# Other instruction durations in the planner that orders a hybrid SSD and attention layer on one core

## The chip, the core and the metric

The kernel runs on one core of one Trainium2 chip. A core has TensorE (matrix products, transposes as products with an identity, weight loads), VectorE (DVE in the rows), ScalarE (ACT), GpSimd (POOL) and SyncE (SP), which here issues all DMAs. The metric is device microseconds of one execution, as the median of several runs. Before the change it is 1239.81 us over 3 runs (1235.19, 1240.91 and 1239.81).

## The reference

For x of 1024 tokens times 1024 channels in float32:

```python
h = layer_norm(x, ln_emb_g, ln_emb_b)
proj = einsum("bsd,de->bse", h, w_in)                # 6688 columns
z, xbc, dt_f, dt_b, q, k, v, g = split(proj)
xbc = silu(centred_dwconv(xbc, conv_w, conv_b))      # 5 taps
y = ssd(forward) + ssd(backward) + D * xs            # 16 heads, 2 groups, 8 chunks of 128 tokens
y_ssm = rms_norm(y * silu(z))                        # per group
w = softmax(s1 - m_h|t-s|) - lam * softmax(s2 - m_h|t-s|)   # 8 heads, two maps each
y_attn = rms_norm(w @ v) * 0.8 * silu(g)
mix = concat([y_ssm, y_attn]) @ w_out
out = layer_norm(ALPHA * h + mix, ln_g, ln_b)
```

## The kernel before

**Products.** Large products are made in float32r, with both operands split into a rounded high part and the remainder: three matmuls of 128x128 by 128x512 stand for one full product (high by high, high by low, low by high). The input projection is 52 blocks of 128 columns; a block is 2 halves of the sequence times 8 slices of 128 channels times 3 matmuls, 48 in all. Transposes, the SSD products and the chunk states are plain float32.

**Lanes.** The work is written as generators, called lanes. `fill` makes the projection blocks one after the other, `weights` loads and splits their weights. In the SSD part `conv`, `states` (the recurrence over chunks, with its state tile H), `maps`, `diag` (products of the within-chunk maps, tile t) and `gate` run for group 0 and then for group 1. In the attention part `scores` makes 128 queries of one head at a time (8 matmuls into the tile sc, for two maps), `combine` subtracts the normalised maps, `values` transposes and splits the result (wh, wl) and multiplies it by the values. `finish` normalises a head. At the end `rows_out`, `y_out`, `residuals` and `project_out` make the output projection: 16 units of 48 matmuls, the first 8 (part 0) on the SSD half, the last 8 (part 1) on the attention half. Part 0 of token blocks 6 and 7 waits for the last head's scores, and part 1 for the last head to be finished.

**The planner.** `Loom.run` decides, while the program is being built, in which order the lanes' instructions are emitted. Every call through an `Engine` wrapper is priced by a cost function (`_pe_cost`, `_dve_cost`, `_act_cost`, `_pool_cost`, `_dma_cost`, in us) and entered by `Loom.note` in a table of when each tile is written. TensorE's clock of the planner is the sum of the prices of what has been emitted on it. On the other engines `Loom.slot` puts an instruction into the first gap that takes it. A lane that yields a tile goes on when the planner's TensorE clock has reached the time the tile is ready plus the lane's margin, from the table LANES (0.2 to 3 us). Among lanes that are ready, the lowest rank goes first:

```python
k = (max(ln[0], now), ln[1], ln[2])          # ready time or now, rank, age
...
ln[0] = ln[5] + max(self.ready.get(t, 0.0) for t in _tiles(...))   # ln[5] is the margin
```

`fill` and the lanes of the output projection have rank 9, the highest number, so they are what TensorE gets while the others wait. All TensorE instructions, and the DVE and ACT ones issued through `VO` and `AO`, keep the order in which they were emitted; other instructions of DVE, ACT and POOL are placed by the framework. The planner never sees the chip: when a price is too low, an instruction of TensorE is emitted whose operand is not there yet on the chip, and TensorE, which works in order, waits.

**What feeds what.** The scores of a head need its q and k blocks. The q and k blocks of head h wait for the scores of head h-2 (`free_since`), its v block for that head's sums, its gate block for its end. At most two sets of maps are between `scores` and the transposes of `values`.

Of the kernel before, what the change touches and what calls it, by code (L numbers as in the profile page):

```python
# [14 lines left out]
ALU = mybir.AluOpType  # L15
PSUM = bass.MemoryType.PSUM
DRAM = bass.MemoryType.DRAM

S = 1024
# [7 lines left out]
ALPHA = 2.0 ** 0.25  # L27
# rank of each lane, and how much later than estimated it takes its inputs to be ready
LANES = dict(weights=(0, 0.8), channels=(1, 1.2), steps=(2, 1.6), z_tail=(2, 0.8), conv=(3, 1), v_tail=(3, 0.4), states=(4.4, 0.8), diag=(4.125, 0.6), maps=(4.4, 0.6), gate=(4.375, 0.2), finish=(4.2, 2), scores=(4, 0.8), combine=(4.125, 0.6), values=(4.25, 0.4), fill=(9, 0.8), rows_out=(9, 0.2), y_out=(9, 3), residuals=(9, 2), project_out=(9, 2))
# [10 lines left out]
def _width(ap):  # L40
    n = 1
    for s in ap.shape[1:]:
        n *= s
    return n


class Loom:
    """Weaves lanes of work into one instruction order.

    A lane is a generator that emits instructions and yields in between: nothing (it can go on),  # L50
    a tile (it can go on once the tile's last write is done), a function (once it holds) or a
    time (it lets other lanes go first for so long).
    When each tile is ready is estimated from the instructions emitted so far; the lane that
    goes on is the first one, by rank, that would not make TensorE wait."""

# [29 lines left out]
    def slot(self, key, start, cost):  # L85
        """The first gap of an engine that takes an instruction ready at start."""
        busy = self.busy.setdefault(key, [])
        i = len(busy)
        while i and busy[i - 1][1] > start:
            i -= 1  # L90
        while i < len(busy) and busy[i][0] - start < cost:
            start = max(start, busy[i][1])
            i += 1
        busy.insert(i, (start, start + cost))
        del busy[:-300]
        return start
# [33 lines left out]
class Engine:  # L130
    """An engine whose instructions are noted in the loom."""

# [20 lines left out]
class Pool:  # L153
    """A tile pool whose slots' reuse is noted in the loom; under are the pools whose place it takes."""

# [19 lines left out]
def _pe_cost(op, out, ins, func=None):  # L175
    n = _width(out)
    if op == "transpose":
        return 0.107
    if ins[0].dtype == F32R:
        return max(0.107, n * 0.000417 + 0.003)  # L180
    return max(0.214, n * 0.00167)


def _dve_cost(op, out, ins, func=None):
    n = _width(out)
    if op == "reciprocal":
        return 0.06 + n * 0.0083
    if op in ("bn_stats", "tensor_reduce"):
        return 0.06 + _width(ins[0]) * 0.00105
    fast = op in ("tensor_scalar", "tensor_copy") and ins[0].space != PSUM  # L190
    return 0.07 + n * (0.00055 if fast else 0.00105)

# [4 lines left out]
def _act_cost(op, out, ins, func=None, state=[None]):  # L197
    cost = 0.12 + _width(out) * 0.00083
    table = _table.get(func, state[0])
    if table != state[0]:  # L200
        state[0] = table
        cost += 1.3
    return cost


def _pool_cost(op, out, ins, func=None):
    if op == "tensor_scalar":
        return 0.07 + _width(out) * 0.001
    return 0.07 + _width(out) * (0.00225 if func is not ALU.pow else 0.4)

# [6 lines left out]
def hybrid_layer_kernel(  # L217
# [8 lines left out]
    loom = Loom(tc)  # L226
    T = Engine(loom, nc.tensor, "PE", _pe_cost, pinned=True)
    V = Engine(loom, nc.vector, "DVE", _dve_cost)
    A = Engine(loom, nc.scalar, "ACT", _act_cost)
# [25 lines left out]

# [1 line left out]
    ident = const.tile([128, 128], F32, name="ident")  # L257
# [7 lines left out]

    # -|query - key| for every offset of a block of 128 queries
    dist = const.tile([128, 1920], F16, name="dist")

# [1 line left out]
    cols = const.tile([128, 104], F32, name="cols")  # L270
# [6 lines left out]

# [1 line left out]
    h_hi = [[hp.tile([128, 512], F32R, name=f"hh{h}_{k}") for k in range(KB)] for h in range(2)]  # L279
# [16 lines left out]
    class Block:  # L296
        """128 projected channels; evac(half, psum) takes each half of the sequence."""

# [7 lines left out]
    def weights():  # L306
        """Loads and splits the weights of a block while the one before it is computed."""
        for n in range(NB):
            yield lambda: len(queue) > n
            b = queue[n]  # L310
            if b.w:
                continue
            before = queue[n - 1]
            yield lambda: before.begun > 0
            sts = []
            for i in range(2):
                st, src = stage_w(b.col, i, wp, 2)
                yield st
                dma(st, src)
                sts.append(st)  # L320
            if not before.pair:
                yield lambda: before.begun > 1
            for st in sts:
                hi, lo = places_w()
                yield (st, hi)
                b.w.append(split_w(st, hi, lo))
# [40 lines left out]

    # ================= embedding LayerNorm and bidirectional SSD =================
    g0x = px.enter_context(ExitStack())
# [29 lines left out]
    def conv_block(b, when, dst_of, after):  # L399
        """Block b of x/B/C: raw projection, then convolution and SiLU into dst_of()."""  # L400
        hold = {}
# [30 lines left out]
    def to_tokens(src, put):  # L432
        """Transposes src [128 ch, S]; put(half, psum [128 tokens, 4, 128])."""
        for half in range(2):
            pt = bank((128, 4, 128))
            yield (src, pt)
            for j in range(4):
                c = 4 * half + j
                transpose(pt[:, j, :], src[:, 128 * c:128 * c + 128])
            put(half, pt)  # L440
# [41 lines left out]
    with tc.tile_pool(name="dp", bufs=1) as dp_, tc.tile_pool(name="p0", bufs=1) as p0_:  # L482
# [93 lines left out]
        def steps_lane():  # L576
            """Step sizes, decays and their sums within chunks."""
            for half in range(2):
# [80 lines left out]
        first = []  # L659
# [35 lines left out]
    def ssd(g):  # L695
# [72 lines left out]
        def maps():  # L768
            """Within-chunk maps of one head, four chunks at a time."""
            loaded = []  # L770
# [94 lines left out]

    # ================= differential attention =================
    ex = px.enter_context(ExitStack())
# [15 lines left out]
    def free_since(h, what, n):  # L883
        """The tiles that head h overwrites are read no more."""
        if h == 0 and what != "done":
            return None
        if h < 2:
            return lambda: state["open"]
        return lambda: getattr(heads_[h - 2], what) == n
# [87 lines left out]
    def scores():  # L977
        """Unnormalised maps of 128 queries at a time."""
        for h, H in enumerate(heads_):
# [32 lines left out]
    def combine():  # L1012
        """Difference of the two normalised maps, left in the first."""
        for _ in range(64):
# [14 lines left out]
    def values():  # L1029
        """Maps transposed and split; weighted sums of the values, 256 queries at a time."""  # L1030
        for _ in range(64):
# [34 lines left out]
    def finish(H, o, half):  # L1066
        """RMS norm over the head's 128 channels, gate, store."""
        h = heads_.index(H)
# [33 lines left out]

    # ================= output projection and LayerNorm =================
    NE = 5
    last = heads_[7]

    def late_rows():
        """Places for the rows of the attention half: tiles of the last head, as they fall free."""
        for tag, shape, bufs, when in (
# [14 lines left out]
    def early_rows():  # L1124
        """The rows for the SSD half take the place of the normalised input."""
        for i in range(16):
            half, j = i // 8, i % 8
            yield lambda: h_used[half] > j
            yield tuple(hp.tile([128, 512], F32R, name=f"o{c}{i}", tag=f"h{c}{half}_{j}") for c in "hl")
# [3 lines left out]
    def rows_out():  # L1133
        """Splits the rows of the output projection, half a row at a time."""
        yield lambda: h_used[0] > 0
# [27 lines left out]
    def y_out():  # L1163
        """Splits the gated outputs of one unit, two units ahead of the products."""
        for tb, part in units:
# [19 lines left out]
    def residuals():  # L1185
        """ALPHA times the normalised input, token blocks in the order of their use."""
        yield lambda: "pool" in res
# [53 lines left out]
    def project_out():  # L1241
        """One unit is 128 tokens times half of the rows; the first NE blocks leave PSUM in between."""
        acc = {}
# [70 lines left out]
```

## Time and profile before

| | |
|---|---|
| median of 3 runs | 1239.81 us (1235.19 to 1240.91) |
| span of the profiled execution | 1236.1 us; the profile has no other time for it |
| instructions | 16398 |
| PE busy | 1176.0 us, 95% |
| PEld busy | 922.4 us, 75% |
| DVE busy | 933.8 us, 76% |
| ACT busy | 677.8 us, 55% |
| POOL busy | 479.9 us, 39% |
| mean granted TensorE clock | 0.990 |

PE is the matmul side of TensorE, PEld its weight loads, which overlap the matmuls. A matmul's length in the trace is its latency; how far apart matmuls follow one another is read from their start times. The granted clock is a share of full speed, averaged over a stretch. All instructions recorded by the wrappers carry one line, 140, so groups are told apart by their tiles. "bk" and "sb" are banks of PSUM.

### The profile page before, as it was taken

What the parts mean: (1) busy time and instruction counts of PE and PEld (TensorE: products, weight loads), DVE (VectorE), ACT (ScalarE), POOL (GpSimd) and SP (SyncE); (2) the same over time, 40 slices, a digit from 0 to 9 for tenths busy, and PEclk for the clock granted to TensorE, in tenths of its full rate; (3) what the DMA queues carried; (4) which work ended last, traced back from release to release, by engine and by line L of the source; (5) the groups of instructions that cost most, each with busy time, mean ns of one, the idle gap of its engine ahead of it and who ended that gap; (6) DMA issues with size and microseconds to landing.
All of it is one profiled execution on the core that took longest, in us unless ns stands there. A gap on an engine that the chain in (4) does not pass through costs nothing. (4 is left out here: it accounts for less than half of the span.)

```text
span 1236.1 us, 16398 instructions
## 1 busy us (share of the span) xinstructions
PE 1176.0 (95%) x5881; PEld 922.4 (75%) x5881; DVE 933.8 (76%) x1334; ACT 677.8 (55%) x1181; POOL 479.9 (39%) x404
## 2 busy tenths in 40 slices
PE   5998999899899999999999999999999998999997
PEld 3787666788567777777787777877777776778885
DVE  6687888867988568788788787887878889962334
ACT  4556356734457456665755656556656687641221
POOL 7422664323654323223332333233332429541354
PEclk9999999999899999999999999999999998999999
DMA  6113335522245421012112111121111263233221
GB/s 198 32 33 112 89 112 167 178 69 65 89 118 151 132 72 49 26 44 51 26 35 52 43 44 35 34 52 35 43 28 47 81 209 107 55 123 112 78 85 60
DMA packets 107591, 98.03 MB, mean 79 GB/s; under 512 B 9364, under 2 KB 79349, under 8 KB 107509
## 3 DMA queue, kind: packets, MB, share of 16 engines
q1 hardware_dynamic: 107509, 96.98, 27.2%
q8 instruction: 46, 0.75, 0.2%
q14 instruction: 36, 0.29, 0.1%
HBM read 75.85 MB, written 16.91 MB: 75 GB/s over the span
## 5 line engine op out<-in xcount | busy, mean ns | idle before, releaser
L140 PE MATMUL bk<-hh,whi 128*128 128x512 f32 x832 | 353.2, 425 | 0.6
L140 PE MATMUL bk<-hl,whi 128*128 128x512 f32 x832 | 327.0, 393 | 3.2 <-POOL hl L140 2.8
L140 PE MATMUL bk<-hh,wlo 128*128 128x512 f32 x832 | 328.0, 394 | 0.0
L140 ACT ACTIVATE p<-p,nm 128x1024 f32<-128x1024 f32 x128 | 146.8, 1148 | 121.7 <-DVE nm L140 121.0
L140 POOL TENSOR_TENSOR wlo<-wst,whi 128x512 fp32r<-128x512 f32 x104 | 161.5, 1557 | 126.9 <-ACT whi L140 109.2
L140 POOL TENSOR_SCALAR p<-p,rs 128x1024 f32<-128x1024 f32 x56 | 64.5, 1152 | 350.4 <-DVE rs L140 287.5
L140 PEld LDWEIGHTS bk<-hh,wlo 128*128 128x128 f32 x832 | 156.6, 188 | 34.9
L140 PEld LDWEIGHTS bk<-hl,whi 128*128 128x128 f32 x832 | 157.7, 190 | 32.9 <-POOL hl L140 5.4
L140 PEld LDWEIGHTS bk<-hh,whi 128*128 128x128 f32 x832 | 157.7, 190 | 32.7 <-issue 5.8
L140 DVE CUSTOM_DVE_ANT_0 p<-sc,dist 128x1024 f32<-128x1024 f32 x128 | 151.3, 1218 | 11.6 <-PE sc L140 10.9
L140 DVE SCALAR_TENSOR_TENSOR p<-p,rs,p 128x1024 f32<-128x1024 f32 x64 | 128.4, 2007 | 22.1 <-POOL p L140 18.0
L140 DVE TENSOR_TENSOR wl<-bk,wh 128x512 fp32r<-128x512 f32 x128 | 87.0, 684 | 15.6 <-ACT wh L140 13.7
L140 ACT CAST wh<-bk 128x512 fp32r<-128x512 f32 x128 | 74.1, 580 | 43.2 <-PE bk L140 42.7
L140 ACT CAST whi<-wst 128x512 fp32r<-128x512 f32 x104 | 64.2, 620 | 46.9 <-PE bk L140 38.1
L140 PE MATMUL bk<-ident,p 128*128 128x128 f32 x512 | 79.4, 278 | 4.7 <-DVE wl L140 2.7
L140 PEld LDWEIGHTS bk<-ident,p 128*128 128x128 f32 x512 | 61.6, 142 | 29.5 <-DVE wl L140 6.2
L140 PE MATMUL bk<-wh,vh 128*128 128x256 f32 x256 | 74.6, 291 | 0.0
L140 PE MATMUL bk<-wl,vh 128*128 128x256 f32 x256 | 72.2, 282 | 0.7 <-DVE wl L140 0.7
L140 PE MATMUL sc<-kk,q 128*128 128x512 f32 x256 | 72.3, 393 | 0.0
L140 PE MATMUL bk<-wh,vl 128*128 128x256 f32 x256 | 72.0, 281 | 0.0
L140 ACT ACT_TABLE_LOAD x42 | 53.9, 1283 | 25.5 <-DVE t L140 15.7
L140 PEld LDWEIGHTS bk<-xt,t 128*128 128x128 f32 x256 | 45.8, 192 | 26.5 <-issue 15.0
(217 smaller groups left out, 2188.1 us busy)
## 6 DMA issues: line engine op xcount, KB each, us to landing
wst<-in_w_in_dram SPq DMA_DIRECT2D x104, 256.0 KB, 3.0
t<-acs_d SPq DMA_DIRECT2D x64, 256.0 KB, 3.5
ws<-in_w_out_dram SPq DMA_DIRECT2D x32, 256.0 KB, 3.1
ys<-yd SPq DMA_DIRECT2D x32, 256.0 KB, 3.0
xb<-in_x_dram SPq DMA_DIRECT2D x8, 512.0 KB, 6.2
zd<-zs SPq DMA_DIRECT2D x16, 256.0 KB, 2.5
gz<-zd SPq DMA_DIRECT2D x16, 256.0 KB, 3.3
yd<-ys SPq DMA_DIRECT2D x16, 256.0 KB, 2.8
```

Source lines behind the costliest of these rows:

```text
L140: r = f(*args, **kw)
```

## The change

The four cost functions for TensorE, DVE, ACT and POOL get other numbers. The comments and docstrings are taken out as well (as empty lines, so that line numbers stay). LANES, the lanes themselves, `_dma_cost` and everything that is computed stay as they are; only the order in which the planner emits instructions can differ.

```diff
 def _pe_cost(op, out, ins, func=None):
     n = _width(out)
     if op == "transpose":
-        return 0.107
+        return 0.11
     if ins[0].dtype == F32R:
-        return max(0.107, n * 0.000417 + 0.003)
-    return max(0.214, n * 0.00167)
+        if ins[0].shape[0] == 64:
+            return 0.14
+        return max(0.107, n * 0.00043 + 0.009)
+    return max(0.166, n * 0.00168)
...
     if op == "reciprocal":
-        return 0.06 + n * 0.0083
+        return 0.06 + n * 0.0068
     if op in ("bn_stats", "tensor_reduce"):
-        return 0.06 + _width(ins[0]) * 0.00105
-    fast = op in ("tensor_scalar", "tensor_copy") and ins[0].space != PSUM
-    return 0.07 + n * (0.00055 if fast else 0.00105)
+        return 0.08 + _width(ins[0]) * 0.00118
+    wide = [i for i in ins if _width(i) >= n and n > 4]
+    if op in ("tensor_scalar", "tensor_copy") and ins[0].space != PSUM:
+        return 0.1 + n * 0.0007
+    if len(wide) > 1 and all(i.space != PSUM for i in wide):
+        return 0.1 + n * 0.0015
+    return 0.08 + n * 0.00118
...
-    cost = 0.12 + _width(out) * 0.00083
+    cost = 0.08 + _width(out) * 0.00104
+    if len(ins) > 1:
+        cost += 0.19
...
 def _pool_cost(op, out, ins, func=None):
     if op == "tensor_scalar":
-        return 0.07 + _width(out) * 0.001
-    return 0.07 + _width(out) * (0.00225 if func is not ALU.pow else 0.4)
+        return 0.1 + _width(out) * 0.001
+    return 0.1 + _width(out) * (0.0027 if func is not ALU.pow else 0.4)
```

## Rows read from the trace of the kernel before

**Rows 1.** The page, part 1: busy time, share of the span, instructions.

```profile
PE 1176.0 (95%) x5881; PEld 922.4 (75%) x5881; DVE 933.8 (76%) x1334; ACT 677.8 (55%) x1181; POOL 479.9 (39%) x404
```

**Rows 2.** Waits of PE, 50 to 975 us: us in total, times, longest.

```profile
PE sb L140 <- DVE H L140: 9.1, 8, 2.7
PE bk L140 <- DVE t L140: 5.9, 5, 1.5
PE bk L140 <- ACT xc L140: 3.9, 3, 2.8
PE bk L140 <- DVE ys L140: 1.7, 1, 1.7
PE bk L140 <- DVE q L140: 1.3, 1, 1.3
...
PE bk L140 <- ACT zr L140: 1.0, 1, 1.0
```

**Rows 3.** Waits of PE, 975 us to the end.

```profile
PE bk L140 <- DVE wl L140: 3.4, 3, 2.5
PE bk L140 <- DVE xr L140: 3.3, 1, 3.3
```

**Rows 4.** Stretches of 25 us: busy (instructions) of five engines, clock, DMA.

```profile
125.00:150.00 25.00, 22.27 (x110) 16.45 (x108) 22.22 (x31) 9.45 (x19) 14.93 (x12) 0.93 0.31 89
...
300.00:325.00 25.00, 21.76 (x98) 15.29 (x97) 23.18 (x30) 8.99 (x17) 16.75 (x12) 0.91 0.28 85
325.00:350.00 25.00, 23.30 (x91) 15.88 (x90) 19.83 (x23) 12.13 (x24) 13.69 (x11) 0.95 0.32 94
...
950.00:975.00 25.00, 25.00 (x135) 19.64 (x134) 21.14 (x34) 14.90 (x28) 7.43 (x5) 1.00 0.16 43
...
1025.00:1050.00 25.00, 21.58 (x90) 16.42 (x89) 23.90 (x27) 19.39 (x31) 24.59 (x17) 0.86 0.25 73
...
1075.00:1100.00 25.00, 22.48 (x114) 18.77 (x113) 14.47 (x23) 11.97 (x22) 6.26 (x5) 0.93 0.43 129
```

**Rows 5.** Groups by shape, whole span: busy us, mean ns, idle before, releaser.

```profile
L140 DVE SCALAR_TENSOR_TENSOR p<-p,rs,p 128x1024 f32<-128x1024 f32 x64 | 128.4, 2007 | 22.1 <-POOL p L140 18.0 <-ACT p L140 4.0
L140 DVE TENSOR_TENSOR wl<-bk,wh 128x512 fp32r<-128x512 f32 x128 | 87.0, 684 | 15.6 <-ACT wh L140 13.7
L140 DVE SCALAR_TENSOR_TENSOR xc<-raw,cols,xc 128x1024 f32<-128x1024 f32 x32 | 47.6, 1488 | 0.9
L140 DVE TENSOR_TENSOR xw<-xt,wend 128x512 f32<-128x512 f32 x28 | 29.1, 1041 | 5.7 <-ACT xt L140 4.9 <-PE sb L140 0.8
```

**Rows 6.** DVE in order of time, 135 to 146 us: start, length, operation.

```profile
135.60 1.53 DVE L140 TENSOR_TENSOR yt<-xt,dc 128x512 f32<-128x512 f32 x1
...
140.18 2.98 DVE L140 TENSOR_TENSOR yt<-xt,dc 128x512 f32<-128x512 f32 x2
143.09 0.68 DVE L140 TENSOR_TENSOR t<-t,nacs 128x512 f32<-128x512 f32 x1
...
144.90 0.67 DVE L140 TENSOR_TENSOR H<-H,sb 128x512 f32<-128x512 f32 x1
```

**Rows 7.** PE in order of time, 100 to 146 us.

```profile
102.30 0.39 PE L140 MATMUL bk<-hh,whi 128*128 128x512 f32 x1
...
110.26 0.39 PE L140 MATMUL bk<-hh,wlo 128*128 128x512 f32 x1
113.42 1.09 PE L140 MATMUL bk<-ident,xc 128*128 128x128 f32 x8 [2.77 <-ACT xc L140]
...
145.62 1.14 PE L140 MATMUL sb<-H,c_ch 128*128 128x512 f32 x2 [2.73 <-DVE H L140]
```

**Rows 8.** Instructions on the tile sc in one stretch: PE, PEld, DVE busy.

```profile
680.00:730.00 50.00, 8.60 (x40) 5.25 (x40) 9.48 (x8) 1.00 0.15 36
```

**Rows 9.** ACT on the tile gate: shortest, median, longest ns, first and last start.

```profile
L140 ACT COPY gate<-bk x16: 563/582/596, 441.8 to 1009.4; 128x512 f32<-128x512 f32 x16
```

**Rows 10.** PE in order of time, 1060 to 1100 us: the last product with values.

```profile
1098.29 0.28 PE L140 MATMUL bk<-wh,vl 128*128 128x256 f32 x1
```

## The prediction, made before the changed kernel was run

> **What bounds the kernel now.** I read the page first: TensorE's matmul side is busy 95% of the span, DVE 76%, and no other engine comes near [rows 1]. So the time is TensorE's work plus what TensorE waits, and an order can only change the second. Then I read the span in stretches of 25 us to see where the missing 60 us (1236.1 less 1176.0) lie. In the attention part, some 450 to 975 us, a stretch has 24.8 to 25.0 us of PE; one stands for 21 of them [rows 4]. Nothing is to be had there. The gaps lie at both ends, which the planner hardly touches (the first products need x, the last norm needs the last product), in the two SSD parts (125 to 225 and 300 to 400 us) and where attention ends (975 to 1100 us).
>
> The waits of PE say for what. From 50 to 975 us they come to 24.2 us in eight kinds, six of which are shown [rows 2]; from 975 us on to 9.1 us in five kinds, two of which are shown [rows 3]. The reader is to see that the large ones are waits for DVE: the recurrence state H, the maps t, the outputs ys, the queries q, together 18.0 us. The convolution (xc, 3.9 us) waits for ACT, which waits for four DVE taps. To these comes the clock. In five stretches the granted clock is below 1 between the levels of 2.4 and 1.2 GHz [rows 4]; each holds or follows a gap of 2.5 us or more. What that costs, as (1 less clock) times 25 us: 1.75, 2.25, 1.25, 3.5 and 1.75, together 10.5 us. So the change has at most some 43 us to win (24.2, 9.1 and 10.5), in places where `fill` or `project_out` has work that could stand in the gap.
>
> **The change part by part.** No instruction is added or removed. What moves is the order, through these prices (formula of the diff, before to after, against the row):
> - A projection matmul, 512 columns: 0.2165 to 0.229 us. On the chip 35 of them take 7.96 us, 0.2274 each [rows 7].
> - DVE, 512 wide from PSUM: 0.608 to 0.684; measured 0.684 [rows 5].
> - DVE, 512 wide with two SBUF operands: 0.608 to 0.868; measured 1.041 in the mean for xw [rows 5], from 0.68 to 1.49 [rows 6].
> - DVE, 1024 wide with two SBUF operands: 1.145 to 1.636; measured 1.488 for a tap, 2.007 for the combined map [rows 5].
> - ACT, 512 wide: 0.545 to 0.612; 1024 wide with a bias: 0.97 to 1.335. POOL, 512 wide and two operands: 1.222 to 1.482.
> - Eight matmuls of a score block: 1.73 to 1.476 (four of 0.229, four of 0.14); measured 8.60/5 = 1.72 [rows 8]. This one gets worse, by a quarter of a us per block, less than any margin of its successors; I cost it at nothing.
>
> *The waits for DVE in the SSD parts.* I work out one of them, the 2.73 us before the product with H at 145.62 [rows 7]. DVE had run without a gap through eleven instructions from 135.60 to 145.57, 9.97 us, of which the first, two in the middle, one without a neighbour and the last are shown [rows 6]. Seven of them are 512 wide with two SBUF operands, three 512 wide from PSUM, one 256 wide from PSUM. The planner counts 10 x 0.608 + 0.339 = 6.42 us before, 7 x 0.868 + 3 x 0.684 + 0.382 = 8.51 after. It covers these with TensorE work by its own price: 6.42 x 0.2274/0.2165 = 6.74 us of chip time before, 8.51 x 0.2274/0.229 = 8.45 after. The shortfall against 9.97 falls from 3.23 to 1.52, so 53% is closed. Over all 18.0 us of such waits: 9.5 us.
>
> *The convolution.* A tensor_scalar, four taps and the SiLU count 0.633 + 4 x 1.145 + 0.97 = 6.18 before and 0.817 + 4 x 1.636 + 1.145 = 8.51 after; as chip time 6.49 and 8.45, 1.96 us more. The wait of 2.77 us [rows 7] shrinks by that, the two others of together 1.1 vanish: 3.1 us.
>
> *Waits for ACT alone* (zr, vc, o: about 1 us each [rows 2]): the price moves by 0.07; nothing.
>
> *The end of attention.* The wait for xr follows residual rows that POOL prepares (1.222 to 1.482 a piece), that for wl an ACT and a DMA. Bounds: nothing, because the DMA's price stays, to all 6.7 us [rows 3]. I take a third, 2.2 us, since only the POOL and DVE half of the queue is priced better, and not all of it.
>
> *The clock.* In the SSD parts 5.25 us. With 53% of the 2.7 us gaps closed they are 1.3 us long; t and ys waited up to 1.7 us elsewhere [rows 2] without such a fall. Bounds 0 and 5.25; I take half, 2.6. At the end 5.25 us; a third again, 1.7.
>
> *What it may cost.* The order is new everywhere, so some lane will now come early. The nearest row is what the present order pays away from the ends, 33.3 us [rows 2, 3]; the bounds are 0 and that much again. While `fill` has work, a price that is too high costs nothing, for TensorE takes fill instead, and most prices now lie at or above the row except where POOL runs beside. I take 7 us.
>
> Sum: 9.5 + 3.1 + 2.2 + 2.6 + 1.7 - 7 = 12.1 us off the span of 1236.1, so 1224. The median of the runs lies 3.7 us above that span, hence 1228 us.
>
> **The rivals.**
>
> *A. The prices still miss what costs most.* A DVE instruction with two SBUF operands takes 0.68 us alone (143.09, when POOL was idle) and 1.49 when POOL works beside it (140.18) [rows 6]. One price, 0.868, is too high for the one and too low for the other, and the long gaps come where the POOL ones meet: seven such at 1.49 would be 10.4 where 6.1 is counted. Then the H waits keep most of their length, the clock falls as before, and what is won (the conv, half of the shorter waits: 3.1 + 4) is paid back by new waits of 7 us. That gives 1236 to 1240, no change. Against it: even in the worked chain the mean was below 1.1 us. The Trainium skill, GPSIMD Engine Reference, section Key points, says that GpSimd shares its SBUF interfaces with VectorE and contends with instructions that have two SBUF inputs; the trace agrees (0.68 against 1.49 us). Taken as the rule of this kernel it would give A, 1238 us. The chance of A by the rows is 0.22.
>
> *B. Attention falls behind the fill, and the end runs dry.* This ends on the other side. Per set of maps the counted chain from scores to the split (two reductions over 1024, exp, reciprocal and product, POOL, combine, one evacuation, one remainder) grows from 2.29 + 0.97 + 0.15 + 1.09 + 1.15 + 0.55 + 0.61 = 6.81 to 2.58 + 1.34 + 0.15 + 1.12 + 1.64 + 0.61 + 0.68 = 8.12 us, TensorE's counted work per set only by 0.2. Two sets are in flight, so if the chain sets the pace, a set comes 0.65 us later, and twice that where DVE queues. The pace is now 10 us, five blocks in 50 us, evenly [rows 8], which speaks for a chain that sets it; that PE stays full and that fill is still at work when only six score blocks are left (the last gate block ends at 1009.4 [rows 9]; I count six score products after it) speaks against. Slowed by 0.5 to 1.1 us over 58 sets, fill ends with 3 to 6 more sets open. After it a set takes some 11 us (1009.4 to 1098.3 [rows 9, 10] for eight) with 4 us of products of its own, so each needs 7 us of `project_out`. After 1098.3 some 130 us of products follow, 11.7 units at 11 us: eight of part 1 and 3.7 of part 0, of which two wait for the last scores. So 1.7 units, 19 us, are free: three more sets fit, six lack 42 - 19 = 23 us. Then 1224 + 23 + 3.7, about 1250 us. It decides from the fourth set on. Chance 0.18.
>
> *C. Nearly everything closes.* The margins of LANES come on top of prices that are now right, so the waits of the SSD parts and the clock with them go: 24.2 + 5.25, half of the end (9.1 + 5.25)/2, no new waits beyond 12. That is 25 us, 1215. Chance 0.12.
>
> **How the numbers follow.** The forecast has 0.48, A 0.22, B 0.18, C 0.12. Likeliest time 1228 us, its own range 1219 to 1236. The range that holds 8 in 10 takes in C's edge and most of B: 1213 to 1248. A measurement of this kernel tells 0.5%, 6 us, from no change: below 1233.6 is faster, above 1246.0 slower. Faster: most of the forecast (0.43) and C, 0.55. Same: A with the forecast's upper edge and B's light end, 0.27. Slower: the rest of B and new waits at their upper bound, 0.18.
>
> **What would show it.** Right: the attention stretches unchanged at 25 us; waits for H and t in the SSD parts at half or less; no wait for xc over 1 us; clock 1.00 at 125 to 150 and 300 to 350 us; the last gate block earlier by about what the SSD parts won. A shows as the same H waits, each with POOL beside DVE. B shows as more than nine score blocks after the last gate block, and PE idle between 1050 and 1130 us. The forecast is wrong if the SSD waits stay, if the attention part loses its full TensorE, or if a new wait of several us appears at the change from one part to the next.

## The result, and the profile after

The changed kernel takes 1317.83 us in the median of 4 runs (1313.44 to 1325.8), against 1240.36 for the kernel before on the same chip (4 runs): a ratio of 1.064, 95% interval 1.0605 to 1.0676. The prediction said 1228, with 1248 as the upper end of its range. The direction is wrong. The profiled execution has a span of 1316.0 us against 1236.1, 79.9 us more, at a mean clock of 0.964 against 0.990.

The page of the kernel after, part 1 (answers to [rows 1]):

```profile
PE 1198.4 (91%) x5881; PEld 940.7 (71%) x5881; DVE 904.4 (69%) x1334; ACT 671.4 (51%) x1173; POOL 469.3 (36%) x404
```

The same 5881 products are made. TensorE is busy 22.4 us longer, at a lower mean clock (how much of it the clock makes was not separated), and idle 57.5 us longer. To see where, I cut both spans at two events: the first set of maps that DVE takes from PSUM, and the last product of the projection. The rows are stretches: start and end, length, then busy time of PE, PEld, DVE, ACT, POOL, clock, DMA share, GB/s. The kernel before:

```profile
50.00:437.90 387.90, 363.16 (x1709) 279.77 (x1708) 310.39 (x392) 205.58 (x384) 163.93 (x143) 0.99 0.37 109
437.90:1007.80 569.90, 565.51 (x3042) 446.90 (x3041) 460.77 (x690) 354.63 (x617) 175.55 (x130) 1.00 0.18 47
1007.80:1236.10 228.30, 213.47 (x976) 171.26 (x974) 130.33 (x195) 91.53 (x145) 110.08 (x81) 0.97 0.32 100
```

And the kernel after:

```profile
50.00:462.60 412.60, 368.81 (x1694) 284.23 (x1693) 303.02 (x391) 193.86 (x376) 161.41 (x143) 0.94 0.35 103
462.60:1051.80 589.20, 558.20 (x2935) 442.28 (x2934) 416.27 (x645) 338.42 (x582) 162.55 (x125) 0.99 0.17 44
1051.80:1316.00 264.20, 237.15 (x1098) 188.74 (x1096) 152.74 (x239) 112.93 (x181) 114.65 (x86) 0.95 0.28 90
```

All three parts lose: the SSD part 24.7 us, attention while there is projection left 19.3, what follows the last projection product 35.9. In attention TensorE's idle time goes from 4.4 to 31.0 us (length less PE).

What fills TensorE there is the projection. Products that read the tile hh (two of every three projection products) show when it is at work. The rows are PE's share alone; first the kernel before, in two stretches of 80 us:

```profile
640.00:720.00 80.00, 45.66 (x128) 1.00 0.17 40
720.00:800.00 80.00, 45.66 (x128) 1.00 0.16 40
```

then the kernel after, two stretches of one head each and two without projection:

```profile
693.70:780.90 87.20, 43.31 (x128) 0.98 0.15 37
780.90:868.20 87.30, 43.39 (x128) 1.00 0.15 37
...
696.80:715.20 18.40, 0.02 (x1) 0.91 0.06 15
...
421.00:461.00 40.00, 0.51 (x2) 0.59 0.43 137
```

Both kernels spend exactly one head's four blocks (192 products, 128 of them with hh) per head, that is, per 8 sets. Before, that takes 80.0 us. After, it takes 87.2, and for 18.4 us of them there is no projection product at all. Counted in the order of time, the sets of heads 1 to 6 of the kernel before have 12, 30, 33, 27, 12, 30, 30 and 18 projection products between them, the same for every head. Those of heads 3 to 5 after have 21, 57, 30, 33, 3, 0, 0 and 48: the first four sets draw 141 of the 192, and two go without. Such stretches (more than 8 us without a projection product; the kernel before has none after 50 us) begin at 615.8, 696.8, 784.2, 871.6 and 959.4 us, when 14, 21, 29, 37 and 45 sets are scored, and end at the gates, where `free_since` lets the q block of the next head but one begin (sets 16, 24, 32, 40, 48). A sixth and the longest, 421 to 461 us, waits for the pools of attention to be opened: the gate block of head 0 can't begin before. In the kernel before, the first product of that block follows the one ahead of it within 4.4 us (429.8 and 434.2 us).

What TensorE does in such a stretch. PE in order of time, in brackets the idle time and what ended it:

```profile
696.36 0.40 PE L140 MATMUL bk<-hh,wlo 128*128 128x512 f32 x1
...
702.40 0.38 PE L140 MATMUL bk<-wl,vh 128*128 128x256 f32 x1 [1.32 <-DVE wl L140]
...
705.18 1.94 PE L140 MATMUL bk<-ident,p 128*128 128x128 f32 x8 [1.22 <-DVE p L140]
...
710.98 0.50 PE L140 MATMUL bk<-osl,ones_r 128*128 128x512 f32 x1 [1.17 <-DVE osl L140]
...
715.18 0.50 PE L140 MATMUL bk<-hh,whi 128*128 128x512 f32 x1
```

It walks down the chain of one set, one link at a time, and no projection product is left to stand in the gaps. In front of attention it is the same with the end of the SSD part:

```profile
431.89 1.11 PE L140 MATMUL bk<-ident,yt 128*128 128x128 f32 x4 [5.09 <-DVE yt L140]
...
450.34 1.09 PE L140 MATMUL bk<-ident,yt 128*128 128x128 f32 x4 [3.77 <-DVE ms L140]
```

The waits of PE from 50 to 975 us (answers to [rows 2]):

```profile
PE bk L140 <- DVE ms L140: 8.5, 3, 3.8
PE bk L140 <- DVE osl L140: 7.8, 5, 2.3
PE bk L140 <- DVE ys L140: 7.4, 2, 4.8
...
PE bk L140 <- DVE yt L140: 7.0, 5, 5.1
PE bk L140 <- ACT raw L140: 6.1, 1, 6.1
PE bk L140 <- DVE t L140: 5.4, 5, 2.1
...
PE sb L140 <- DVE H L140: 4.0, 4, 2.2
...
PE bk L140 <- ACT xc L140: 0.3, 1, 0.3
```

In this stretch of time the waits add up to 72.4 us instead of 24.2; from 975 us on to 20.7 instead of 9.1. H waits 4.0 us instead of 9.1, xc 0.3 instead of 3.9; of the 5.4 us for t, 5.1 lie in the stretch from 421 to 461 us. The four kinds H, t, ys and q together came to 18.0 us and come to 16.8.

The new waits are of two sorts. The six stretches without projection hold 43 of the 72.4 us: all of ms, osl and p, most of wl, yt and t. The waits for raw and ys are another sort: projection products stand on both sides of them, so `fill` had not run out.

```profile
226.17 0.40 PE L140 MATMUL bk<-hh,wlo 128*128 128x512 f32 x1
226.42 0.66 PE L140 MATMUL bk<-ident,xc 128*128 128x128 f32 x4
233.21 1.12 PE L140 MATMUL bk<-ident,xc 128*128 128x128 f32 x4 [6.13 <-ACT raw L140]
...
234.40 0.77 PE L140 MATMUL bk<-hh,whi 128*128 128x512 f32 x1
```

There a product was emitted before the chip was ready for it, and TensorE stood in front of it. Up to the first set the balance is plain. TensorE's waits come to 24.1 us before and 43.5 after, 19.3 of them in the stretch from 421 to 461 us. The other 24.2 are as many as before, of other kinds: H, t and xc went from 18.9 to 4.7 us, raw and ys from 1.7 to 13.6.

Stretches of 25 us (answers to [rows 4]):

```profile
225.00:250.00 25.00, 18.87 (x85) 15.12 (x84) 16.51 (x22) 9.70 (x19) 9.88 (x9) 0.86 0.36 104
...
300.00:325.00 25.00, 24.24 (x120) 19.49 (x119) 20.10 (x17) 10.15 (x17) 6.17 (x6) 1.00 0.32 90
...
425.00:450.00 25.00, 11.04 (x48) 9.10 (x48) 17.54 (x36) 8.44 (x24) 4.77 (x6) 0.57 0.44 137
450.00:475.00 25.00, 20.53 (x81) 15.13 (x82) 12.80 (x29) 8.61 (x16) 4.50 (x6) 0.75 0.27 95
...
700.00:725.00 25.00, 20.51 (x112) 16.11 (x111) 21.79 (x37) 17.18 (x28) 6.09 (x5) 0.93 0.04 10
...
1050.00:1075.00 25.00, 20.59 (x85) 15.78 (x84) 16.98 (x24) 15.27 (x25) 7.54 (x5) 0.86 0.36 116
```

The clock at 300 us is back at 1.00, as forecast, but 0.86 at 225 us, where the wait for raw lies. At 425 and 450 us it is 0.57 and 0.75; in the first of the two TensorE was idle for 14 of 25 us. Reckoned as in the prediction, that is (0.43 + 0.25) x 25 = 17 us at one place; it is an upper bound, since TensorE stood idle for part of it anyway.

How many sets are left at the last projection product: products that read the keys kk (four per set) after it, before and after.

```profile
1007.80:1236.10 228.30, 6.86 (x24) 0.97 0.32 100
```

```profile
1051.80:1316.00 264.20, 12.28 (x40) 0.95 0.28 90
```

Six sets were open before, ten are now. The last gate block ends at 1054.2 instead of 1009.4 us [rows 9], and the last product with values comes at 1196.85 instead of 1098.29 [rows 10].

### The profile page after: what moved, and what is told of

Same layout as the page of the kernel before. It is cut to its first block, busy times and chain, and to the rows that moved or that the text cites. A ratio compares the mean times of both kernels' runs of the same rounds, so it can differ in the third digit from the quotient of the medians.

```text
span 1316.0 us, 16406 instructions
## 1 busy us (share of the span) xinstructions
PE 1198.4 (91%) x5881; PEld 940.7 (71%) x5881; DVE 904.4 (69%) x1334; ACT 671.4 (51%) x1173; POOL 469.3 (36%) x404
## 5 line engine op out<-in xcount | busy, mean ns | idle before, releaser
L140 POOL TENSOR_TENSOR wlo<-wst,whi 128x512 fp32r<-128x512 f32 x104 | 152.9, 1474 | 206.4 <-ACT whi L140 203.6
L140 DVE SCALAR_TENSOR_TENSOR p<-p,rs,p 128x1024 f32<-128x1024 f32 x64 | 109.4, 1709 | 33.3 <-POOL p L140 28.4
L140 DVE TENSOR_TENSOR wl<-bk,wh 128x512 fp32r<-128x512 f32 x128 | 87.2, 685 | 45.3 <-ACT wh L140 44.0
L140 PEld LDWEIGHTS bk<-ident,p 128*128 128x128 f32 x512 | 63.6, 147 | 31.7 <-issue 18.7
L140 PE MATMUL sc<-kk,q 128*128 128x512 f32 x256 | 80.8, 425 | 4.5 <-DVE nm L140 4.5
L140 ACT ACTIVATE t<-t,nacs 128x128 f32<-128x128 f32 x128 | 41.7, 392 | 44.3 <-DMA t<-acs_d 44.3
## 6 DMA issues: line engine op xcount, KB each, us to landing
wst<-in_w_in_dram SPq DMA_DIRECT2D x104, 256.0 KB, 2.9
t<-acs_d SPq DMA_DIRECT2D x64, 256.0 KB, 3.7
ws<-in_w_out_dram SPq DMA_DIRECT2D x32, 256.0 KB, 2.7
ys<-yd SPq DMA_DIRECT2D x32, 256.0 KB, 3.1
zd<-zs SPq DMA_DIRECT2D x16, 256.0 KB, 2.9
gz<-zd SPq DMA_DIRECT2D x16, 256.0 KB, 3.5
yd<-ys SPq DMA_DIRECT2D x16, 256.0 KB, 2.4
```

The costliest lines, as they stand in the source:

```text
L140: r = f(*args, **kw)
```

## The experiments

T1 is the theory that the traces suggest: with the new prices a chain of DVE and ACT work counts for more TensorE work than before, so the planner spends the projection faster than the gates supply it. T2: the new prices place DVE and ACT work worse. T3: the new TensorE prices emit products too early. T0 came up on the way: any displacement of the order loses, since that of before is a chosen one. Ratios are to the kernel before on the same chip, with 95% intervals.

**Former prices, all margins of LANES 0.3 us longer.** A longer margin draws more fill, as a dearer price does, without touching a price.

```diff
-LANES = dict(weights=(0, 0.8), channels=(1, 1.2), ...
+LANES = dict(weights=(0, 1.1), channels=(1, 1.5), ...
```

> The former prices, and every margin in LANES 0.3 us larger. Theory 1 (the fill runs dry): what slowed the changed kernel is that the counted chain of every lane grew, by 1.3 us per set of maps in attention, so more projection work is put into each wait, the projections run ahead to their gates and TensorE then stands while a chain goes on. A set passes some seven margins, so this adds 2.1 us to the counted chain with no price changed: the same dips at the head boundaries and at the end of the second SSD group, 1290 to 1340 us. Theory 2 (the new prices place the work of DVE and ACT worse, and TensorE waits for that): no price has changed, so 1230 to 1255 us. Theory 3 (the new TensorE prices, 0.14 for the 64-row matmuls above all, emit products too early): as theory 2, 1230 to 1255 us.

Measured: 1287.31 us, 1.040 (1.037 to 1.0434). That is a little below T1's range and far above that of the others. Stretches without projection stand before four of the same gates (671.9, 751.4, 838.4 and 933.4 us), with 54 sets scored at the last fill. No price has to be new for this to happen. The stretch in front of attention, which T1 expected too, is missing: the first set comes at 440.0 us, 2 later than before.

**New prices, margins halved.**

```diff
-LANES = dict(weights=(0, 0.8), channels=(1, 1.2), ...
+LANES = dict(weights=(0, 0.4), channels=(1, 0.6), ...
```

> The new prices, and every margin in LANES halved. The counted chain of a set is then 8.1 + 1.8 = 9.9 us, against 6.8 + 3.6 = 10.4 before and 8.1 + 3.6 = 11.7 after the change. Theory 1: the fill lasts as long as before, attention has full stretches again, 1225 to 1260 us. Theory 2: the prices are as in the changed kernel, so most of the loss stays, 1290 us or more. Theory 3: the same, 1290 us or more.

Measured: 1327.6 us, 1.072 (1.0695 to 1.0746). T1 in its simple form, that price and margin of a chain just add up, falls; T2 and T3, which both said 1290 or more, fit this run. The six stretches without projection stay (120.6 us in all, 125.9 with the whole change), and waits for osl and osh come on top (18.7 and 17.6 us over the span).

**All new prices but DVE's; and TensorE's and DVE's alone.** In one `_dve_cost` is the former, in the other `_act_cost` and `_pool_cost`.

> The new prices for TensorE, ACT and POOL, the former ones for DVE. Theory 1: the chain of a set grows by the 0.4 to 0.5 us of ACT alone, a third of the whole, so a third of the loss or less, 1240 to 1268 us. Theory 2: DVE is placed as before, ACT not; 1240 to 1270 us. Theory 3: all the TensorE prices are in, so 1300 us or more.

> The new prices for TensorE and DVE, the former ones for ACT and POOL. Theory 1: the chain of a set grows by the 0.86 us of DVE, two thirds of the whole, 1265 to 1300 us with dips at the head boundaries. Theory 2: most of the loss comes with DVE, 1270 to 1310 us. Theory 3: 1300 us or more, and as slow as the run with all but DVE.

Measured: 1258.28 us, 1.017 (1.0143 to 1.0192) without DVE's, 1320.38, 1.067 (1.0643 to 1.0695) with TensorE's and DVE's alone, more than expected. T1's and T2's ranges for the first run are nearly the same, and both hold; T3 fails there, though 1320 alone would suit it. Taking DVE's prices out takes most of the loss out, but TensorE's were in both runs, and no run has DVE's new prices alone.

**All new prices, the projection paced in attention.** A slice of heads 1 to 7 waits until the scores have come far enough: 8 slices (24 products) per set.

```diff
+        return steps[0] < 0 + 8 * done["sets"] + 0
...
+                        if blocks[0].col in paced and not may_fill():
+                            yield may_fill
+                        steps[0] += blocks[0].col in paced
```

> All the new prices, and the projection blocks of heads 1 to 7 paced: by the time n sets of maps are scored, no more than 8 n of their slices of three matmuls may have been made, the even share (64 slices and 8 sets a head). The order of the SSD parts stays as in the changed kernel. In the order as emitted, no set from head 1 on is left without fill, where the changed kernel leaves nine of 40 without. Theory 1 (the fill runs dry at its gates): the dips at the head boundaries vanish, the loss up to the first scores (25 us) stays, and fill ends some two sets later, so 1280 to 1300 us. Theory 2 (the new prices place DVE and ACT worse): the waits of TensorE stay, spread over the sets, 1305 us or more.

Measured: 1288.75 us, 1.040 (1.0358 to 1.0444), as T1 expected. With the same prices, holding the projection back wins 29 us: that it runs out at the gates is a cause, and not only a sign. The stretch in front of attention stays as it was (422.0 us, 38.7 long), and 56 sets are scored at the last fill. From the first set on this run still takes 822.7 us, against 853.4 with the whole change and 798.2 before, so pacing gives back 31 of 55 us; TensorE is busy 482.7 of the 500 us from 500 on, not all of them.

**Paced in both parts.** The blocks that fill the second SSD group are held back as well, by the progress of `diag` and `gate`, 16 slices ahead; in attention 16 slices behind.

```diff
+        if steps[0] < 112 and not done.get("open"):
+            return steps[0] < 112 * (sum(G[1].diag) + G[1].gate) / 24 + 16
+        return steps[0] < 112 + 8 * done["sets"] + -16
```

> As the run before, with the pace of attention set back by 16 slices, so that fill ends with the 58th set as in the former kernel, and with the seven blocks that fill the second SSD group paced by its finished maps and gates. Theory 1: the 25 us lost up to the first scores, the 19 us of attention and most of the 36 us after the last fill come back, 1235 to 1258 us. Theory 2: 1290 us or more.

Measured: 1282.31 us, 1.035 (1.0311 to 1.038): missed. What follows the last fill is back to 227.3 us, with 58 sets scored. The SSD part is not mended; its stretch without projection only moved to where the second group starts. PE's products with hh there:

```profile
308.20:333.10 24.90, 0.04 (x1) 0.66 0.14 41
```

The first set comes at 465.9 us, later still than the 462.6 of the whole change.

**New prices, DVE's times 0.7.** Now DVE's prices are lower than the trace has them, and near the former ones.

```diff
+def _dve_cost(op, out, ins, func=None):
+    return 0.7 * _dve_cost0(op, out, ins, func)
```

> All the new prices, with those for DVE multiplied by 0.7, so that its relation to TensorE's is below that of the former prices for wide operations. No set without fill in the order as emitted. Theory 1, with the queue on DVE in the planner as the cause of the long chain: 1235 to 1260 us, attention full. Theory 2: the DVE prices are wrong for every single operation, TensorE meets late operands everywhere, 1270 us or more.

Measured: 1247.15 us, 1.006 (1.0036 to 1.0092). In attention there is no stretch without projection, and it is full (499.4 of 500 us from 500 to 1000); the SSD part has one of 10.3 us (at 153.6). DVE prices lowered by 30% do far better than the new ones, so T2 falls as the account of the whole; the waits for raw and ys above are of its kind. What this run loses, it loses ahead of attention (first set at 455.9, 18.0 us later than before); from there on it takes 790.2 us, 8.0 less than the kernel before. No run joins that half to the former SSD order.

**TensorE's new prices alone.**

> The new TensorE prices alone, all others as before. No set without fill in the order as emitted. Theory 1: within 10 us of the former kernel, 1230 to 1250 us. Theory 3 (the prices of the 64-row matmuls and the small products emit products too early): 1280 us or more, with waits before products of the scores and the maps t.

Measured: 1260.12 us, 1.017 (1.0126 to 1.0213). T3 falls, but T1 missed by 10 us: with TensorE dearer and DVE as before, lanes are counted ready too early, and PE waits for H 14.8 us, for osl 7.1 and for p 6.4.

**New prices, TensorE's times 1.2.**

```diff
+    return 1.2 * _pe_cost0(op, out, ins, func)
```

> All new prices, TensorE's multiplied by 1.2, so that they are 20% above what the trace shows. T1 (the counted length of the chains against the counted work of TensorE decides how fast fill is used up): no set of heads 1 to 5 stands without fill in the emitted order, so no stretch without fill in the attention part, at least 57 sets scored at the last fill; but lanes are now counted ready too early, as with the new TensorE prices alone (1260), so 1245 to 1275 us. T2 (what decides is how true each price is): a TensorE price that is wrong by a fifth on top makes it no better than with the true one, 1300 us or more.

Measured: 1275.86 us, 1.029 (1.0261 to 1.0319), one us over T1's range and well below T2's. Making TensorE's prices, of which that of the projection product was right, wrong by a fifth wins 42 us. As T1 said, no stretch without projection reaches 8 us. But 54 sets, not 57, are scored at the last fill.

**Only one DVE price.** Former prices; an operation under 1024 wide with two SBUF operands gets the new one. This is the price I had blamed most for the H waits.

```diff
+    wide = [i for i in ins if _width(i) >= n and n > 4]
+    if n < 1024 and op not in ('tensor_scalar', 'tensor_copy') and len(wide) > 1 and all(i.space != PSUM for i in wide):
+        return 0.1 + n * 0.0015
```

> Former prices; only a DVE operation under 1024 wide with two SBUF operands gets the new price (0.868 instead of 0.608 us at 512). It is the price that the H chain of the SSD part was missing most, and of the attention chain only the gate and the finish have it. T1: attention stays fed (58 sets scored at the last fill, give or take one), the H waits of 9.1 us fall to 6 or less, 1228 to 1245 us. Rival (any dearer DVE price spends the fill of the SSD part, and the loss before the first set comes back): first set scored 15 us later or more, 1255 us or more.

Measured: 1290.55 us, 1.041 (1.0382 to 1.0442). The rival was right. The H waits did fall, from 9.1 to 6.8 us, and the first set came 19 us later (457.1), 54 sets scored at the last fill. The truer price took 2.3 us off its wait and lost eight times as much up to the first set alone.

**Former prices, margins halved.**

> Former prices, all margins of LANES halved. T1: fill is drawn less, so it lasts at least as long as before (58 sets or more at the last fill, tail 228 us or less), no stretch without fill; the DVE waits of the SSD part grow, since less stands in front of them. 1235 to 1260 us. Rival (the prices of before were already too high somewhere and the margins waste fill): 1230 us or less.

Measured: 1299.69 us, 1.048 (1.0453 to 1.0512): missed by both. Fill lasts (58 sets, 229.2 us after it), but PE waits directly: H 18.5 us, osl 22.9, t 11.3. The margins make up for the former prices' being low.

**ACT's prices alone.**

> Former prices; only ACT's are new (0.545 to 0.612 us at 512 wide, 0.97 to 1.335 for an exp of 1024 with a bias). T1: ACT stands in the chain of each set (exp, split), so the counted chain grows by some 0.4 us per set, and six of the 40 sets of heads 1 to 5 stand without fill in the emitted order: short stretches without fill at the gates of the heads, 1250 to 1275 us. Rival (only DVE, which is the busier engine, carries the loss, and ACT has slack): 1234 to 1246 us.

Measured: 1279.43 us, 1.033 (1.0298 to 1.0361); T1 was near (4 us over its range). Stretches without projection of 10.9, 20.3 and 20.3 us before gates. The prediction had put waits for ACT alone at nothing. With TensorE's and POOL's prices beside them ACT's cost less, not more (1.017 above).

**Four displacements of the order.** Every version so far was slower than the kernel before, those with longer and those with shorter margins too. Hence T0: former prices with margins 0.02 longer, DVE times 1.02, DVE times 1.05, TensorE times 1.05.

> Former prices, every margin of LANES 0.02 us longer. In the emitted order every set of heads 1 to 5 has projection work beside it, 5 to 13 slices of three. T1 (sizes decide, with a tipping point): 1234 to 1248 us. T0 (any displacement of the order loses, since the order of before is a chosen one): 1260 us or more.

> Former prices, DVE's multiplied by 1.02. In the emitted order the slices per set of a head are 13, 5, 13, 12, 12, 6, 13, 6 (sum 80, though a head has 64 with its own; heads differ): none without. T1: not over the tipping point, 1234 to 1250 us. T0: 1260 us or more.

> Former prices, DVE's multiplied by 1.05: in the emitted order the first set after a gate has 24 slices and the last before it 1, so it is just over the tipping point, with less than a fifth of the change that the new DVE prices make. T1: stretches without fill in front of the gates of heads 3 to 7, 54 to 56 sets scored at the last fill, 1260 to 1290 us, though it differs from the run with 1.02 by 3% of one table. T0: as slow as the other three of this call, within 1%.

> Former prices, TensorE's multiplied by 1.05, away from the tipping point: 6 to 14 slices at every set. T1: attention stays fed, 58 sets or more at the last fill; the SSD lanes are counted ready earlier, so the DVE waits there grow by some us, 1240 to 1258 us (the new TensorE prices alone gave 1260). T0: 1260 us or more, no better than DVE 5% up.

Measured: 1241.66 us, 1.001 (0.9992 to 1.0032); 1261.84, 1.018 (1.0137 to 1.0229); 1259.92, 1.015 (1.0112 to 1.0189); 1267.01, 1.021 (1.0165 to 1.0252). T0 is wrong for the smallest displacement and right for the other two that T1 let off: 2% on one table costs 1.8%, with projection at every set and 58 scored at the last fill. That run pays in waits for wl (16.3 us over the span against 3.4) and xr (8.1 against 3.3); the one with dearer TensorE in the SSD part (first set at 458.3 us; xc 12.8, H 11.9, t 10.3). DVE times 1.05 shows the loss at the end nearly by itself: first set at 442.6, 54 sets at the last fill, then 256.0 us against 228.3. Of what T1 expected of it, one set per head (the seventh of heads 2 to 5) has no projection product beside it, but no stretch there reaches 8 us. So a displaced order alone cost from nothing to 2.1% in these runs, with no rule seen in how much; how much of that is in the 6.4% of the whole change is not shown.

**The change in two parts of the planning.** The new prices hold up to one point of the planning, or from there on. Each cost function picks its table by the flag.

```diff
     g0x.close()
+    _part["att"] = True
```

The expectations speak of the end of the SSD part, but the flag is set earlier: after the gate of the first SSD group, before `ssd(1)` is planned. TensorE's order in the one run leaves that of the whole change at 335 us, in the other it leaves that of before at 300 us. So the second SSD group is planned with attention's prices in both.

> New prices until the SSD part is emitted, former ones from there on. T1 (the loss is made in each part by the prices that hold there): first set scored some 25 us later than before (462 instead of 438), the stretch of some 40 us without fill in front of attention as with the whole change; then attention as before, 58 sets scored at the last fill, tail 225 to 232 us, 1258 to 1272 us. Rival (the SSD order hands attention a wrong start, on which the later loss rests): stretches without fill in front of the gates of the heads, 1290 us or more.

> Former prices until the SSD part is emitted, new ones from there on. T1: first set scored at 438 us as before, then stretches without fill in front of the gates of the heads and 54 sets at the last fill as with the whole change, 1285 to 1302 us, so that both runs' losses add up to the 78 us of the whole. Rival (the later loss rests on the SSD order): 1250 us or less.

Measured: 1259.17 us, 1.017 (1.0134 to 1.02), and 1303.43, 1.054 (1.0504 to 1.0566). Stretches by the same events, new prices up to that point:

```profile
50.00:452.80 402.80, 367.03 (x1697) 282.13 (x1696) 301.16 (x391) 191.54 (x374) 162.57 (x143) 0.96 0.37 105
452.80:1026.00 573.20, 567.50 (x3055) 449.26 (x3054) 458.20 (x690) 355.08 (x617) 178.53 (x130) 1.00 0.18 46
1026.00:1253.30 227.30, 210.99 (x976) 168.60 (x974) 128.46 (x195) 91.49 (x145) 109.60 (x81) 0.99 0.32 100
```

and new prices from that point on:

```profile
50.00:444.40 394.40, 361.80 (x1701) 277.77 (x1699) 301.81 (x392) 207.90 (x386) 164.85 (x143) 0.98 0.38 108
444.40:1033.20 588.80, 557.60 (x2931) 442.46 (x2930) 416.34 (x645) 338.63 (x582) 162.48 (x125) 0.99 0.17 44
1033.20:1297.00 263.80, 236.91 (x1098) 188.17 (x1096) 152.60 (x239) 112.99 (x181) 114.73 (x86) 0.95 0.29 90
```

Attention and the end separate cleanly. With the former prices there they are as before to 3.3 us, although the first set comes 15 us late; with the new ones they are as in the whole change to 0.4 us, although it comes 18 us earlier than there. Their loss is made by the prices that hold in them. The spans lose 17.2 and 60.9 us, together 78.1 of 79.9.

Ahead of attention the expectations missed: the first set comes at 452.8 and 444.4 us (462 and 438 were expected), and the stretch in front of attention is 13.9 and 15.8 us long, against 40.0 with all the new prices. New prices in the first group cost 14.9 us, in the second 6.5; of the whole, 24.7, they give 21.4. The waits for raw and ys belong to the first group's prices: 6.3 and 7.1 us in the first run, none and 1.7 in the second.

## Why the prediction was wrong

**The step that failed** is "What it may cost": "While `fill` has work, a price that is too high costs nothing, for TensorE takes fill instead." The condition is the mistake. Fill has no work at a closed gate, and there is one in front of attention and one for each head from head 2 on (heads count from 0). A head brings 192 products; what its first four sets draw beyond their share is missing from the later ones. I had asked what a wrong price does to one wait, and not what all prices together do to the supply. The term was put at 7 us, with 33.3 as its upper bound. TensorE's waits from 50 us on went from 33.3 us to 93.1, and 44 us of the new sum stand in the six stretches without projection. Two of the prediction's signs of being wrong came: attention lost its full TensorE, and new waits of several us (5.1 for yt, 3.8 for ms) stand at the change from one part to the next.

**"Nothing is to be had there"** (attention) was right for a gain and was taken to hold for a loss too. Stretches at 24.8 to 25.0 us of PE [rows 4] showed a balance of draw and supply, and I read them as a reserve. This part and what follows it make 55 of the 80 us.

**Rival B** named the mechanism (a longer counted chain, fill that ends with more sets open, PE idle after it), with four more sets open, inside its 3 to 6, and its sign of PE idle after 1050 us is there. It went wrong in place and price: it let fill run out once, at the end, where it runs out in front of attention and of the gates of heads 3 to 7; and it held 19 us at the end to be free. The end grew by 35.9 us for four sets: PE is busy 23.7 us longer (four sets of some 4 us make 16 of that; the clock is 0.95 instead of 0.97) and idle 12.2 longer. Nothing of the 19 us showed.

**The H waits**: forecast to shrink by 53%, shrank by 56% (9.1 to 4.0); xc by 3.1 us, shrank by 3.6; the clock at 300 us went to 1.00 as said; and outside the stretch in front of attention t went from 5.9 to 0.3. For these waits the step was right. The 9.5 us of the sum did not come, though: it spread the one worked chain over all 18.0 us of H, t, ys and q, and these still come to 16.8, since ys grew by 5.7 and t waits in the new stretch. What H, t and xc won up to the first set, 14.2 us, the waits for raw and ys took back by growing 11.9, and the stretch in front of attention added 19.3.

**ACT at nothing** was wrong for the same reason as the whole: it looked at waits for ACT, while the price also enters the counted length of the chains that ACT stands in (1.033 by itself).

**Rival A** (prices that miss what costs most) was wrong on the H waits, which closed. Its other half, that what is won is paid back by new waits, came true in the SSD part (raw and ys), but that makes none of the 80 us: it cancels the gain.

**What stays open.** Why the planner draws 141 products into four sets with the new prices is argued, not shown: counted chains are longer by 19% (6.81 to 8.12 us), TensorE's counted work by little, so more rank 9 work fits in front of each ready time. With halved margins it did not go away, so a sum over one chain doesn't explain it; that DVE's queue inside the planner lengthens the chains is my reading, and no run tests it. Up to the first set the waits outside the long stretch are as many as before, so the 24.7 us are, but for rounding, that stretch (some 19) and 5.7 us more of busy TensorE; but no run gives them back, for pacing the second SSD group only moved the stretch. With attention paced, 24.5 of the 55.2 us from the first set on remain, and their cause is open. DVE's new prices alone were not run. No version beat the kernel before; the nearest are margins 0.02 longer (1.001) and DVE's prices times 0.7 (1.006).

## What to carry to other kernels

A greedy planner's prices and margins are one tuned set: when filler work is rationed by gates, a dearer price of the work it waits for can spend the ration faster, and a price may be truer and the order worse. Before changing prices, count the filler between consecutive consumers and compare it with what each gate supplies; a part where the bounding engine is full can't gain, but it can lose what keeps it full. And try several displacements of a per cent or two first, before reading a meaning into the new prices: here three of four cost 1.5 to 2.1%, and one nothing.

## What the runs showed of the hardware

The combined map, 128x1024 with two SBUF operands, has mainly two durations, and the share of them moves with the order. DVE on the tile p (shortest, median and longest ns), before and after; the means are 2007 [rows 5] and 1709:

```profile
L140 DVE SCALAR_TENSOR_TENSOR p<-p,rs,p x64: 1268/2298/2350, 443.4 to 1082.5; 128x1024 f32<-128x1024 f32 x64
```

```profile
L140 DVE SCALAR_TENSOR_TENSOR p<-p,rs,p x64: 1265/1285/2403, 467.8 to 1183.1; 128x1024 f32<-128x1024 f32 x64
```

Two of them, DVE in order of time:

```profile
703.75 1.28 DVE L140 SCALAR_TENSOR_TENSOR p<-p,rs,p 128x1024 f32<-128x1024 f32 x1 [1.14 <-POOL p L140]
...
708.02 2.29 DVE L140 SCALAR_TENSOR_TENSOR p<-p,rs,p 128x1024 f32<-128x1024 f32 x1
```

and POOL beside them:

```profile
702.59 1.12 POOL L140 TENSOR_SCALAR p<-p,rs 128x1024 f32<-128x1024 f32 x1 [4.00 <-DVE rs L140]
...
707.96 1.28 POOL L140 TENSOR_TENSOR o<-o,gate 128x512 f32<-128x512 f32 x1
```

Alone it takes 1.28 us, beside 1.28 us of POOL 2.29, longer by 1.01 us or four fifths of what POOL runs. The Trainium skill, GPSIMD Engine Reference, section Key points, says that GpSimd shares its SBUF interfaces with VectorE and contends with instructions that have two SBUF inputs; the trace agrees and adds the price. An update of H, 128x512 with one operand in PSUM, shows the contrast: 20 of 24 ran beside a POOL instruction in the kernel before and took 0.67 to 0.69 us, the 4 alone 0.67 to 0.68. The new price of the combined map, 1.636 us, is met by neither of its cases. In the kernel before most run beside POOL (the median is the long one), in the kernel after most run alone. That is 19 of the 29 us by which DVE's work got shorter, 904.4 us against 933.8, while the kernel got longer.
